# A transformer block on one core: separate PSUM banks for maxima and scores, a one-row shift, two issue tracks for the delta rule, and all weight subtractions on GpSimd

## The chip, the core and the metric

The kernel runs on one core of one Trainium2 chip. A core has TensorE for matrix products (PE in the profile, its weight loads PEld), VectorE (DVE), ScalarE (ACT), GpSimd (POOL) and SyncE, which issues most DMAs (SP). Each engine works through its own list of instructions, in the order in which the program emits them. The metric is the device time of one execution in microseconds (us). Before the change the median of three runs is 3656.62 us (3653.87 to 3657.88).

## The reference

One block of a diffusion transformer: 2048 latent tokens of width 1024, and 256 context tokens. The input is normalised and modulated, projected, and goes through two groups of heads side by side; their outputs are concatenated and projected, and a gated MLP with a width-3 convolution follows.

```
# (a) softmax attention: 8 query heads of 64, 2 key/value heads, blocks of 128 queries
s = einsum("bqkgd,bskd->bkgqs", q_blk, k)        # k: 256 context + 2048 latent keys
p = softmax(s, axis=-1)
o = einsum("bkgqs,bskd->bqkgd", p, v)

# (b) delta rule: 4 heads of 128, forwards and backwards, chunks (64 in the reference)
lower = einsum("bhnid,bhnjd->bhnij", k_beta, k) * decay_strict
t_inv = triangular_solve(lower + eye, eye)       # inverse of a unit triangular matrix
u, w = t_inv @ (v * beta), t_inv @ (k_beta * exp(g_cum))
v_new     = u_n - w_n @ state                    # chunk after chunk
new_state = state * d_n + k_n.T @ v_new
o_n       = q_n @ state + intra @ v_new
```

The inverse of a chunk needs only that chunk's keys and decays. The state goes from chunk to chunk.

## The kernel before, in words

**Stages.** About the first 700 us make the projections, the convolutions and the modulation. The stage that the change touches follows: attention and delta rule together, from about 725 to 1923 us. Then come the output projection and the MLP, which the change leaves alone.

**A planner draws up the order.** In the stage of the change no engine's program is written by hand. `attention` (L1097) and `delta` (L1282) only record operations in a `Plan` (L192). `Plan.cost` (L226) books a duration for each operation: on VectorE 65 ns and the elements at 0.96 per ns, fewer if an input allows a fast mode; on ScalarE 50 ns and 0.836 ns for an element, 42 more if the input lies in SBUF, 93 more if scale or bias is a tensor. `Plan.order` (L303) lays all operations out on the five engines by these durations, by the tiles that are free and by urgency. Every operation belongs to a *track*: `a` (attention), whose urgency is the share of its TensorE work still to do, and `d0` and `d1` (delta rule forwards and backwards), whose urgency is 1.35 (`DW`) times the rest of their longest path. Buffers of one ring are given out in the order of the program within a track (L355). `Plan.issue` (L398) then emits the instructions in the order of their planned starts. That is why nearly all rows of the stage carry line L403 in the profile: operations are told apart by their tiles' names.

**PSUM.** There are 8 banks of 128 x 512 f32. `RINGS` (L44) gives ring `s` two tiles of two banks each, `g` three single banks, `o` one. Scores (`sc`) and the products for the maxima (`sm`, `sm_rest`) both take their tiles from `s`.

**Attention.** 16 query blocks and 2 key heads make 32 groups of 4 heads. For each group `tops` (L1176) first makes a row maximum over all 2304 keys with a one-pass product: eight tiles of 128 x 1024 and a rest, each reduced by VectorE to `mx`, and then `top`. `top` is scaled, split into two f16 parts (`sh6`, `sh2`), turned into rows by TensorE (`tp`) and copied by ScalarE to two rows of `qx` (L1198 to L1210). The score product has two passes, `kh` x `qt` and `kx` x `qx`; the two rows of `qx` meet two constant rows of `kx` and so subtract the maximum. For each of nine score tiles of a group (two key tiles of 128 keys, 512 columns each, L1228) ScalarE makes `p = exp(esc * sc + shift)`, with `esc` and `shift` from tiles. The weights are split in f16: `hp` is the rounded value (VectorE for tiles 0, 3, 6, ScalarE for the others) and `lp = p - hp` (VectorE for tiles 1, 4, 7, `LO_V`, GpSimd for the others). `ops` collects 24 small products for a tile. After each score tile's `exp` one piece of the next group's `tops` is recorded (`next(ahead)`, L1236); what is left of it follows behind the ninth tile.

**Delta rule.** 18 chunks of 128 tokens in each direction. Of every chunk: loads `tT` (keys and queries, turned), `tk` (keys and values) and `rws` (decay rows), one buffer each and direction; decays (`pdb`, `db`), the product of keys (`pkk`), the lower matrix in two f16 parts (`lh`, `ll`), first 2 x 2 inverses (`m0`, `tt`, `t`); then six levels that double the block, each with `py` on TensorE, a masked copy to `y` on VectorE, `pa` on TensorE, and two copies by ScalarE of half of `t` and half of `tt` (L1397, L1398); then one correction step: `it = i16 - t` on VectorE, `pr` on TensorE, `r = it + pr` on VectorE, `pn`, and `ti`, the inverse. The rest is the state: `pw`, `rv`, `pv`, `vn`, `pz`, the new state `s`, and the output `po`. Tiles `ti`, `rv`, `vn`, `o` share a ring of two.

## Time and profile before

| | |
|---|---|
| median of three runs | 3656.62 us (3653.87 to 3657.88) |
| the profiled execution | 3658.18 us |
| its span, first to last instruction | 3656.3 us |
| granted TensorE clock, mean over the span | 0.972 |
| TensorE (PE) busy | 3407.5 us |
| VectorE (DVE) busy | 2466.2 us |
| ScalarE (ACT) busy | 1708.3 us |
| GpSimd (POOL) busy | 1221.0 us |

A row of grouped instructions reads: line, engine, operation, output and inputs by the program's tile names, shapes, count; then busy time in us, mean ns of one; then the idle time of that engine just before them and what ended it. A row of waits reads: who waited, for whom, us in total, times, longest. In a row of a stretch each engine has its busy time and, in brackets, its instructions, and at the end stand granted clock, DMA share and GB/s. Ends of TensorE instructions are modelled in the profile; their starts are measured.

### The profile page before, as it was taken

To read this page: it belongs to the slowest core of one execution; us is meant where nothing else is said; L and a number is where in the kernel's file an instruction comes from. 1 tells how busy PE (TensorE), PEld (TensorE's weight loads), DVE (VectorE), ACT (ScalarE), POOL (GpSimd) and SP (SyncE) were. 2 spreads that over 40 slices of the span, in tenths; PEclk is the share of its full clock that TensorE was granted. 3 is DMA by queue.
4 is the path that set the end of the run, shared out by engine and by line. 5 is a ranking of instruction groups with operands and counts; after the bars stand their busy time and mean duration, and the time that the engine had idled before them with its cause. 6 is when DMAs were issued, how large, how long until landed. Compare 5 with 4: busy or idle time off the path is not lost.

```text
span 3656.3 us, 65344 instructions
## 1 busy us (share of the span) xinstructions
PE 3407.5 (93%) x26245; PEld 2735.9 (75%) x26245; DVE 2466.2 (67%) x3589; ACT 1708.3 (47%) x2772; POOL 1221.0 (33%) x1327
## 2 busy tenths in 40 slices
PE   7899999889989899999887889999999999999998
PEld 3799888766666666666656668888888888888898
DVE  5664778888778887878775657753775376537653
ACT  5442343466667676667663444332433243324331
POOL 4684555434444454544455531100110010001100
PEclk8899999999999999999998999999999999999999
DMA  6222445711111121211105662334333433343333
GB/s 223 85 72 89 137 119 167 211 40 49 62 61 39 56 63 61 65 44 58 58 25 187 222 231 94 98 110 126 117 98 112 125 120 96 113 126 116 98 101 96
DMA packets 209200, 381.31 MB, mean 104 GB/s; under 512 B 20360, under 2 KB 95720, under 8 KB 208624
## 3 DMA queue, kind: packets, MB, share of 16 engines
q1 hardware_dynamic: 207056, 371.74, 32.2%
q0 software_dynamic: 1840, 5.39, 0.6%
q8 instruction: 206, 3.38, 0.4%
q14 instruction: 98, 0.80, 0.1%
HBM read 297.73 MB, written 79.72 MB: 103 GB/s over the span
## 4 chain that ended last, share of the span: by engine, by line
PE 67%; DVE 16%; POOL 5%; DMA 4%; ACT 4%; issue 4%; SPq 0%; POOLq 0%; DVEq 0%; ACTq 0%
PE pu L520 8%; PE pu L521 8%; PE pu L519 8%; PE sc L403 5%; PE pdn L520 4%; PE pdn L521 4%; PE pdn L519 4%; PE ops L403 3%; PE po L403 3%; DVE mx L403 3%; PE sm L403 2%; ACT p L403 2%; DVE lp L403 1%; PE pg L520 1%; PE pg L519 1%
## 5 line engine op out<-in xcount | busy, mean ns | idle before, releaser
L403 POOL TENSOR_TENSOR lp<-p,hp 128x1024 f16<-128x1024 f32 x192 | 412.0, 2146 | 515.3 <-ACT hp L403 246.8
L519 PE MATMUL pu<-h,ws_u 128*128 128x512 f32 x1408 | 552.0, 392 | 2.1 <-ACT h L403 2.1
L520 PE MATMUL pu<-h,ws_u 128*128 128x512 f32 x1408 | 550.3, 391 | 2.5 <-DVE h L403 2.5
L521 PE MATMUL pu<-h,ws_u 128*128 128x512 f32 x1408 | 549.9, 391 | 0.0
L403 ACT ACTIVATE p<-sc,shift,esc 128x1024 f32<-128x1024 f32 x288 | 347.5, 1207 | 171.7 <-PE sc L403 165.3
L403 DVE TENSOR_REDUCE mx<-sm 128x2 f32<-128x1024 f32 x256 | 312.2, 1220 | 74.8 <-PE sm L403 74.1
L1715 POOL COPY carry<-ue 128x2 f32<-128x2 f32 x132 | 24.9, 189 | 893.5 <-ACT ue L1713 893.5
L520 PEld LDWEIGHTS pu<-h,ws_u 128*128 128x128 f32 x1408 | 265.3, 188 | 60.1 <-DVE h L403 4.5
L519 PEld LDWEIGHTS pu<-h,ws_u 128*128 128x128 f32 x1408 | 265.4, 188 | 59.0 <-ACT h L403 3.5
L521 PE MATMUL pdn<-hid,ws_d 128*128 128x512 f32 (+2 forms) x880 | 307.5, 349 | 0.0
L520 PE MATMUL pdn<-hid,ws_d 128*128 128x512 f32 (+2 forms) x880 | 307.5, 349 | 0.0
L521 PEld LDWEIGHTS pu<-h,ws_u 128*128 128x128 f32 x1408 | 265.4, 189 | 55.0
L519 PE MATMUL pdn<-hid,ws_d 128*128 128x512 f32 (+2 forms) x880 | 306.5, 348 | 0.0
L1713 ACT COPY ue<-pu 128x512 f32<-128x512 f32 x176 | 103.2, 587 | 370.1 <-PE pu L521 369.3
L1724 DVE SCALAR_TENSOR_TENSOR cv<-ue,cols,cv 128x512 f32<-128x512 f32 (+1 forms) x352 | 264.9, 753 | 15.8 <-DVE cv L1721 0.5
L403 PE MATMUL sc<-q,kh 128*128 128x512 f16 x576 | 225.0, 391 | 11.4 <-ACT p L403 8.8
L403 PE MATMUL sc<-qx,kx 128*128 128x512 f16 x576 | 225.1, 391 | 2.9 <-ACT qx L403 2.8
L1687 DVE TENSOR_TENSOR ws_u<-raw_u,ws_u 128x1024 fp32r<-128x1024 f32 x176 | 214.6, 1219 | 17.4 <-ACT ws_u L1682 17.4
L1721 DVE TENSOR_SCALAR cv<-ue,cols 128x512 f32<-128x512 f32 (+1 forms) x176 | 96.4, 548 | 190.4 <-ACT ue L1713 188.1
L1687 DVE TENSOR_TENSOR ws_d<-raw_d,ws_d 128x1024 fp32r<-128x1024 f32 (+1 forms) x96 | 109.0, 1136 | 157.7 <-ACT ws_d L1682 155.6
L403 ACT CAST hp<-p 128x1024 f16<-128x1024 f32 x192 | 201.8, 1051 | 5.7 <-PE ops L403 1.5
L403 PE MATMUL ops<-vst,hp 128*128 128x65 f16 (+1 forms) x4608 | 192.1, 194 | 9.0 <-ACT hp L403 6.2
(582 smaller groups left out, 8178.4 us busy)
## 6 DMA issues: line engine op xcount, KB each, us to landing
raw_u<-in_wu SPq DMA_DIRECT2D x176, 512.0 KB
raw_d<-in_wd SPq DMA_DIRECT2D x64, 512.0 KB
tk<-gsc SPq DMA_DIRECT2D x34, 512.0 KB
tT<-gsc SPq DMA_DIRECT2D x66, 256.0 KB
wm<-in_wm SPq DMA_DIRECT2D x64, 256.0 KB
gsc<-kd SPq DMA_DIRECT2D x64, 256.0 KB
raw_o<-in_wo SPq DMA_DIRECT2D x32, 512.0 KB
raw_d<-in_wd SPq DMA_DIRECT2D x32, 384.0 KB
```

Source lines behind the costliest of these rows:

```text
L403: fn(**{k: v.get() if isinstance(v, Lazy) else v for k, v in kw.items()})
L519: PE.matmul(out=ps, lhsT=hi_l(k), rhs=hi_r(k), start=st, stop=False)
L520: PE.matmul(out=ps, lhsT=hi_l(k), rhs=lo_r(k), start=False, stop=False)
L521: PE.matmul(out=ps, lhsT=lo_l(k), rhs=hi_r(k), start=False, stop=en)
L1687: V.tensor_tensor(out=made[u][:, 1, :n], in0=raws[u][:, :n], in1=made[u][:, 0, :n].bitcast(F32), op=ALU.subtract)
L1713: S.copy(out=ue[:, 2:514], in_=ps)
L1715: G.tensor_copy(out=carry[:, b, :], in_=ue[:, 512:514])
L1721: V.tensor_scalar(out=cv[:, :W], in0=ue[:, 0:W], scalar1=fw[0], scalar2=cols[:, C_FB + b:C_FB + b + 1], op0=ALU.mult, op1=ALU.add)
L1724: V.scalar_tensor_tensor(out=cv[:, :W], in0=ue[:, i:i + W], scalar=fw[i], in1=cv[:, :W], op0=ALU.mult, op1=ALU.add)
```

## The change

Seven edits, all in the stage of attention and delta rule but for two scalings of constant rows ahead of it. They come together:

1. **Banks.** Ring `s` has one tile of two banks, for scores alone. A new ring `m` has two single banks, for the maxima: 16 products of 512 columns and 2 rests for a group, each with a reduction of 512 columns, in place of 8 and 1 of 1024.
2. **Recording.** Behind each of the first two score tiles two pieces of `tops` are recorded, so that a group's `tops` ends ahead of its ninth score tile.
3. **Shift.** `top` itself is turned by TensorE, one row in place of two; ScalarE scales it and adds the constant shift when it copies it to one row of `qx`. Four VectorE operations on 128 x 4 values for each group go. Key rows carry the whole scale, so `exp` has a constant scale and no bias.
4. **Subtractions.** `lp = p - hp` is on GpSimd for all nine tiles.
5. **Inverse.** The two copies of a level become one of 512 elements with a strided output. `it` goes; a product with minus the identity (`n16`) puts `-t` into `pr`, and `r = pr + i16`.
6. **Tracks.** What a chunk does up to `ti` is recorded in tracks `i0` and `i1`, the state in `d0` and `d1`, all four with weight 1.35. `tT` and `tk` have two buffers, `ti` a ring of two of its own.
7. **Booked durations.** VectorE 150 ns, 200 more for a fast mode and 55 for a tensor scalar; ScalarE 170 ns, 25 more for an input in SBUF; TensorE 2.34 columns per ns in place of 2.3. This holds in this stage alone.

```diff
-RINGS = dict(s=2, o=1, g=3, p=4, hp=4, lp=4, q=2, h=4, fa=1, at=1, fb=2, tT=1, tk=1, st=2, t=2, fin=1)
+RINGS = dict(s=1, m=2, o=1, g=3, p=4, hp=4, lp=4, q=2, h=4, fa=1, at=1, fb=2, tT=2, tk=2, st=2, t=2, ti=2, rw=1, fin=1)
...
-            return 65 + n / 0.96 / fast + 65 * at, 0.0
+            return fixed[0] + n / 0.96 / fast + fixed[1] * at + (fixed[2] if fast > 1 else 0), 0.0
...
-            return 50 + n * 0.836 + (225 if "accum_out" in kw else 0) + (0 if src(kw["in_"]) else 42) + 93 * at, 0.0
+            return fixed[3] + n * 0.836 + (225 if "accum_out" in kw else 0) + (0 if src(kw["in_"]) else fixed[4]) + 93 * at, 0.0
...
-    plan.patience, plan.rate = PATIENCE, 2.3
+    plan.patience, plan.rate, plan.fixed = PATIENCE, 2.34, (150, 55, 200, 170, 25)
...
+            for h in range(GR):
+                for j in range(4):
+                    sps = psum(f"sm_{nm}_{h}_{j}", "m")
+                    lead(sps, h, 4 * j, 4 * j + 4)
+                    V.tensor_reduce(out=mx[:, h, j:j + 1], in_=sps, axis=AX, op=ALU.max)
+                    if j % 2: yield
             for h in range(0, GR, 2):
-                for j in range(4):
-                    sps = two_banks(f"sm_{nm}_{h}_{j}")
-                    with plan.group():
-                        for i in range(2):
-                            lead(sps[:, i], h + i, 4 * j, 4 * j + 4)
-                    V.tensor_reduce(out=mx[:, h:h + 2, j], in_=sps, axis=AX, op=ALU.max)
-                    yield
...
+                sps = psum(f"sm_{nm}_rest{h}", "m")
...
             V.tensor_reduce(out=top, in_=mx, axis=AX, op=ALU.max)
-            V.tensor_scalar(out=top, in0=top, scalar1=-1.0 / ROWV, scalar2=None, op0=ALU.mult)
...
-            V.tensor_copy(out=sh6, in_=top)
-            V.tensor_copy(out=sh2[:, :, 0], in_=sh6)
-            V.tensor_tensor(out=sh2[:, :, 1], in0=top, in1=sh6, op=ALU.subtract)
...
-                    PE.transpose(out=tps[0:2, h * P:(h + 1) * P], in_=sh2[:, h, :], identity=ident)
-            S.copy(out=qx[0:2, g * GR:(g + 1) * GR, :], in_=tps[0:2, :].rearrange("p (h t) -> p h t", t=P))
+                    PE.transpose(out=tps[0:1, h * P:(h + 1) * P], in_=top[:, h:h + 1], identity=ident)
+            S.activation(out=qx[0:1, g * GR:(g + 1) * GR, :], in_=tps[0:1, :].rearrange("p (h t) -> p h t", t=P),
+                         func=AF.Identity, scale=-1.0 / ROWV, bias=shift[0:1])
...
-                S.activation(out=pr, in_=sps, func=AF.Exp, scale=esc, bias=shift)
-                next(ahead, None)
+                S.activation(out=pr, in_=sps, func=AF.Exp, scale=1.0 / SC)
+                for _ in range(2 if c0 < 4 else 1):
+                    next(ahead, None)
...
-                (V if c0 // 2 in LO_V else G).tensor_tensor(out=lp, in0=pr, in1=hp, op=ALU.subtract)
+                G.tensor_tensor(out=lp, in0=pr, in1=hp, op=ALU.subtract)
...
-    FT = {n: (t, RINGS[t]) for t, ns in (("fa", "db qe"), ("at", "at"), ("fb", "ti rv vn o")) for n in ns.split()}
+    FT = {n: (t, RINGS[t]) for t, ns in (("fa", "db qe"), ("at", "at"), ("ti", "ti"), ("fb", "rv vn o")) for n in ns.split()}
...
+            def two_halves(b):
+                step = 512 + (2 * d - 1) * b
+                x = both_t[:, (1 - d) * b:(1 - d) * b + 2 * step].rearrange("p (a c b) -> p a c b", a=2, b=b)
+                return x[:, :, 0:512 // b - 1:2, :]
...
-                S.copy(out=half(t, b, 1 - d), in_=cols_of(pa[:, 0:256], b))
-                S.copy(out=half(tt, b, d), in_=cols_of(pa[:, 256:512], b))
-            it = f16t("it")
-            V.tensor_tensor(out=it, in0=i16, in1=t, op=ALU.subtract)
+                S.copy(out=two_halves(b), in_=pa.rearrange("p (a c b) -> p a c b", a=2, b=b))
             pr = bank("pr")
             with plan.group():
+                PE.matmul(out=pr, lhsT=n16, rhs=t, start=True, stop=False)
...
-            V.tensor_tensor(out=r, in0=it, in1=pr, op=ALU.add)
+            V.tensor_tensor(out=r, in0=pr, in1=i16, op=ALU.add)
...
+            plan.track = f"d{d}"
             rv = tk[:, 1, :]
...
-            plan.track = f"d{d}"
+            plan.track = f"i{d}"
             next(both[d])
-    plan.issue(dict(a=("work", 1.0), d0=("path", DW), d1=("path", DW, STAG)))
+    plan.issue(dict(a=("work", 1.0), i0=("path", IW), i1=("path", IW, STAG), d0=("path", DW), d1=("path", DW, STAG)))
```

More of the change, by code (lines that the diff above doesn't have):

```diff
@@ L225, in cost @@
     @staticmethod
-    def cost(eng, name, kw, rate):
+    def cost(eng, name, kw, rate, fixed):
         def src(x):
@@ L295, in add @@
             op.behind.add(self.gate)
-        d, a = self.cost(eng, name, kw, self.rate)
+        d, a = self.cost(eng, name, kw, self.rate, self.fixed)
         op.calls.append((fn, kw))
@@ L725, in front @@
         V.tensor_scalar(out=gm, in0=gm, scalar1=1e-15, scalar2=None, op0=ALU.max)
-        ginv = mk(wk, [P, 2], F32, "ginv", "ginv", 1)
-        V.reciprocal(out=ginv, in_=gm)
-        for i, o in enumerate((R_Q, R_K)):
-            V.tensor_scalar(out=rows[:, o:o + HD], in0=rows[:, o:o + HD], scalar1=ginv[:, i:i + 1], scalar2=GTOP,
+        ginv = mk(wk, [P, 1], F32, "ginv", "ginv", 1)
+        V.reciprocal(out=ginv, in_=gm[:, 0:1])
+        for o, by, sc in ((R_Q, ginv, GTOP), (R_K, gm[:, 0:1], SC / GTOP)):
+            V.tensor_scalar(out=rows[:, o:o + HD], in0=rows[:, o:o + HD], scalar1=by, scalar2=sc,
                             op0=ALU.mult, op1=ALU.mult)
@@ L1078 @@
     G.dma_start(out=lv16, in_=k32_d[:, K_LV:K_END])
+    n16 = c2.tile([P, P], F16, name="n16")
+    V.tensor_scalar(out=n16, in0=ident, scalar1=-1.0, scalar2=None, op0=ALU.mult)
     for h in range(HG):
@@ L1135, in attention @@
                             scalar2=None, op0=ALU.mult)
-            V.tensor_scalar(out=kx[0:2, :, g, :], in0=ones[0:2, :].unsqueeze(1).broadcast_to([2, NCK, P]), scalar1=ROWV, scalar2=None, op0=ALU.mult)
+            V.tensor_scalar(out=kx[0:1, :, g, :], in0=ones[0:1, :].unsqueeze(1).broadcast_to([1, NCK, P]), scalar1=ROWV, scalar2=None, op0=ALU.mult)
         for a in range(0, NCK, 6):
             G.dma_start(out=kx[64:128, a:a + 6], in_=ksc[a:a + 6].rearrange("c p f t -> p c f t")[64:128])
-        esc = plan.tile(ak, [P, 1], F32, "esc", "esc", 1)
-        V.scalar_tensor_tensor(out=esc, in0=gm[:, 0:1], scalar=1.0 / GTOP ** 2, in1=gm[:, 1:2], op0=ALU.mult, op1=ALU.mult)
         shift = plan.tile(ak, [P, 1], F32, "shift", "shift", 1)
-        V.tensor_scalar(out=shift, in0=esc, scalar1=-GTOP ** 2 / 128, scalar2=PSHIFT, op0=ALU.mult, op1=ALU.add)
+        V.scalar_tensor_tensor(out=shift, in0=gm[:, 0:1], scalar=8.0 * SC / 1024, in1=gm[:, 1:2], op0=ALU.mult, op1=ALU.mult)
+        V.tensor_scalar(out=shift, in0=shift, scalar1=PSLACK * SC, scalar2=-1.0 / ROWV, op0=ALU.min, op1=ALU.mult)
+        V.tensor_scalar(out=shift, in0=shift, scalar1=PSHIFT * SC / ROWV, scalar2=None, op0=ALU.add)
         vst = plan.tile(ak, [P, NCK, KV, VW], F16, "vst", "vst", 1)
@@ L1182, in lead @@
                 PE.matmul(out=out, lhsT=qt[:, g * GR + h, :], rhs=kh[:, a:b, g, :], start=True, stop=True)
-            for h in range(0, GR, 2):
-                for j in range(4):
-                    sps = two_banks(f"sm_{nm}_{h}_{j}")
-                    with plan.group():
-                        for i in range(2):
-                            lead(sps[:, i], h + i, 4 * j, 4 * j + 4)
-                    V.tensor_reduce(out=mx[:, h:h + 2, j], in_=sps, axis=AX, op=ALU.max)
-                    yield
-            sps = two_banks(f"sm_{nm}_rest")
-            with plan.group():
-                for h in range(GR):
-                    lead(sps[:, h // 2, 256 * (h % 2):256 * (h % 2) + 256], h, 16, NCK)
-            V.tensor_reduce(out=mx[:, :, 4], in_=sps.rearrange("p a (b t) -> p (a b) t", b=2), axis=AX, op=ALU.max)
+            for h in range(GR):
[4 more added lines that the diff above has]
+                    if j % 2: yield
+            for h in range(0, GR, 2):
+                sps = psum(f"sm_{nm}_rest{h}", "m")
+                with plan.group():
+                    for i in range(2):
+                        lead(sps[:, 256 * i:256 * i + 256], h + i, 16, NCK)
+                V.tensor_reduce(out=mx[:, h:h + 2, 4], in_=sps.rearrange("p (b t) -> p b t", b=2), axis=AX, op=ALU.max)
             yield
@@ L1308, in delta @@
             q.dma_start(out=tk, in_=gsc[ck, :, 1 + 2 * d:3 + 2 * d, :])
-            rws = plan.tile(gs, [12, HG, 3, P], BF16, f"rows{d}", f"rows_{nm}", 1)
+            rws = plan.tile(gs, [12, HG, 3, P], BF16, f"rows{d}", f"rows_{nm}", RINGS["rw"])
             q.dma_start(out=rws, in_=rsc[d, ck].rearrange("h r s t -> r h (s t)"))
```

25 lines of the change are left out of this document (12 added, 13 removed).

## The prediction

> **What bounds the kernel now.** The page first, for the span, and then the busy time of the one stage that changes, cut where the delta rule ends.
>
> ```profile
> span 3656.3 us, 65344 instructions
> 725.00:1867.00 1142.00, 1030.58 (x13829) 759.12 (x13830) 920.69 (x1336) 771.21 (x1144) 514.73 (x281) 0.96 0.18 55
> 1867.00:1923.00 56.00, 42.52 (x544) 25.99 (x541) 38.70 (x40) 36.70 (x38) 34.69 (x20) 0.91 0.10 25
> sum 1198.00, PE 1073.10 PEld 785.11 DVE 959.39 ACT 807.91 POOL 549.42; mean PE 536.55 PEld 392.56 DVE 479.70 ACT 403.96 POOL 274.71
> ```
>
> The columns are PE, PEld, DVE, ACT, POOL. The stage takes 1198 us; PE is busy for 1073, DVE for 959, ACT for 808, POOL for 549. The cuts come from two tiles: the last `fin` is the delta rule's last result, the last `p` attention's last score tile.
>
> ```profile
> L403 DVE TENSOR_TENSOR fin<-po,fin x16: 677/691/693, 1352.3 to 1867.0; 128x512 f32<-128x512 f32 x16
> L403 ACT ACTIVATE p<-sc,shift,esc x288: 1190/1204/1280, 751.2 to 1916.5; 128x1024 f32<-128x1024 f32 x144
> ```
>
> So attention ends last, 56 us behind the delta rule. PE is nearest to its limit, with 1198 - 1073 = 125 us idle. The waits of the stage, for PE, say for whom:
>
> ```profile
> PE pt L403 <- DVE t L403: 26.1, 26, 2.4
> PE tp L403 <- DVE sh L403: 23.9, 16, 2.6
> PE pa L403 <- DVE y L403: 11.0, 18, 1.8
> PE sc L403 <- ACT p L403: 8.8, 20, 1.0
> PE sm L403 <- DVE mx L403: 6.6, 13, 1.5
> PE ops L403 <- ACT hp L403: 6.2, 12, 0.9
> PE ops L403 <- POOL lp L403: 5.5, 6, 2.4
> ```
>
> DVE has the largest share, 68 us in four rows. PE's idle time is larger than its rows say, because ends are modelled. The timeline shows it:
>
> ```profile
> 1414.97 0.38 PE L403 MATMUL sc<-q,kh 128*128 128x512 f16 x1
> 1415.19 0.38 PE L403 MATMUL sc<-qx,kx 128*128 128x512 f16 x1
> ```
>
> Products of 512 columns start 0.22 us apart but are drawn 0.38 long; so every wait hides some 0.16 us more. The stage is thus PE work plus waits of PE, and a gain must come out of the waits.
>
> Why DVE is late is in its own rows:
>
> ```profile
> L403 DVE TENSOR_TENSOR m<-lh,lv x36: 409/1072/1943, 740.2 to 1822.5; 128x512 f16<-128x512 f16 x36
> L403 DVE TENSOR_TENSOR t<-i,m x36: 407/1202/2044, 741.7 to 1825.0; 128x512 f16<-128x512 f16 x36
> L403 DVE CAST hp<-p x96: 671/684/1993, 754.2 to 1914.5; 128x1024 f16<-128x1024 f32 x96
> L403 DVE TENSOR_REDUCE mx<-sm 128x2 f32<-128x1024 f32 x256 | 312.2, 1220 | 74.8 <-PE sm L403 74.1
> L403 DVE TENSOR_REDUCE mx<-sm_rest 128x4 f32<-128x1024 f32 x32 | 39.0, 1218 | 4.9 <-PE sm_rest L403 4.7
> L403 DVE TENSOR_TENSOR lp<-p,hp 128x1024 f16<-128x1024 f32 x96 | 134.4, 1400 | 16.9 <-ACT hp L403 14.4 <-POOL lp L403 1.1 <-PE sc L403 0.6
> L403 DVE CAST hp<-p 128x1024 f16<-128x1024 f32 x96 | 73.7, 768 | 7.8 <-ACT p L403 7.6
> L403 DVE TENSOR_TENSOR t<-i,m 128x512 f16<-128x512 f16 x36 | 37.3, 1035 | 0.5
> L403 DVE TENSOR_TENSOR m<-lh,lv 128x512 f16<-128x512 f16 x36 | 36.2, 1005 | 4.3 <-ACT lh L403 4.0
> L403 DVE TENSOR_SCALAR top<-top 128x4 f32<-128x4 f32 x32 | 29.4, 919 | 0.8
> L403 DVE TENSOR_TENSOR it<-i,t 128x512 f16<-128x512 f16 x36 | 27.4, 764 | 2.2 <-ACT t L403 2.2
> L403 DVE CAST sh<-top 128x4 f16<-128x4 f32 x32 | 16.6, 518 | 0.9
> L403 DVE CAST sh<-sh 128x4 f32<-128x4 f16 x32 | 8.1, 253 | 1.0
> L403 DVE TENSOR_TENSOR sh<-top,sh 128x4 f32<-128x4 f32 x32 | 5.0, 156 | 0.0
> L403 DVE TENSOR_REDUCE oss<-osg 128x4 f32<-128x512 f32 x16 | 10.9, 679 | 2.4 <-ACT osg L403 2.4
> L403 POOL TENSOR_TENSOR lp<-p,hp 128x1024 f16<-128x1024 f32 x192 | 412.0, 2146 | 515.3 <-ACT hp L403 246.8 <-DVE hp L403 222.7 <-PE sm L403 28.9
> ```
>
> The first three rows give min/median/max in ns: `m` takes 409 or up to 1943. `top` scales 4 numbers and takes 919 on average. `mx`, which reads PSUM, hardly varies. So some DVE operations that read SBUF alone stand still for up to about 2 us, one POOL subtraction of 2146 ns.
>
> **The change, part by part.** The ACT rows and two chain pieces that it needs:
>
> ```profile
> L403 ACT ACTIVATE p<-sc,shift,esc 128x1024 f32<-128x1024 f32 x288 | 347.5, 1207 | 171.7 <-PE sc L403 165.3 <-POOL tT L403 1.4 <-DVE mx L403 1.3
> L403 ACT CAST t<-pa 128x256 f16<-128x256 f32 x432 | 137.2, 380 | 30.6 <-PE pa L403 28.0
> L403 ACT CAST t<-pt 128x512 f16<-128x512 f32 x36 | 21.0, 583 | 28.6 <-PE pt L403 28.4
> L403 ACT ACTIVATE db<-pdb 128x512 f32<-128x512 f32 x36 | 21.5, 597 | 25.5 <-PE pdb L403 25.4
> L403 ACT CAST hp<-p 128x1024 f16<-128x1024 f32 x192 | 201.8, 1051 | 5.7 <-PE ops L403 1.5
> 1535.74 4.21 DMA osm<-fin
> 1540.44 3.17 DMA tT<-gsc
> ```
>
> *Engine time.* DVE loses `lp` 134, `top` and three `sh` 29 + 17 + 8 + 5 = 59, `it` 27: 220 us. It gains halves of reductions: 32 x 18 = 576 of about 679 ns (row `oss`, also 512 columns) are 391 us against 312 + 39 = 351, so +40. Net -180. POOL gains 96 x 2.146 = 206 and goes to 755 us, 63% of the stage; the DVE operations that stand still for POOL (`m`, `t`, `hp`) then lose more. Their excess is (1005 - 409) x 36 + (1035 - 407) x 36 + (768 - 684) x 96 = 21 + 23 + 8 = 52 us; times 755/549 it is 72, +20. DVE ends near 800 us. ACT: an `exp` of 512 without tensors takes 597, and 256 columns more cost 583 - 380 = 203, so 1024 take 597 + 406 = 1003 in place of 1207, 288 x 0.204 = 59 us less; copies go from 137 (the row's busy time, in which pairs overlap) to 216 x 583 = 126, 11 less. PE gains 36 products of 512 columns, 36 x 0.22 = 8 us.
>
> *On PE's path.* Each term with the value taken and both ends:
> - Shift: four operations (1846 ns for a group) leave the chain `mx`, `top`, `tp`, `qx`, and `tops` ends one score tile earlier, so work lies behind it. Of 23.9 I take -22; ends -27 and 0. If that cover is gone, each group pays `top` to `qx` in full and the 23.9 stay.
> - Maxima: own banks end `sm` waiting behind scores. Of 6.6 I take -5; ends -8 and +10, the latter if the 40 us of longer reductions lie a quarter on the path.
> - Other DVE waits: `pa` <- `y` falls with DVE's load, -6. `pt` <- `t` is set by POOL, and a planner that books 200 ns more puts `pt` later: 0, ends -20 and +18 (the 20 us above).
> - ACT: of `sc` <- `p`, `ops` <- `hp` (15) -10; ends -20 and 0. What is queued behind a late `exp` is `hp` and the copies of a level.
> - Loads of `tT` and `tk` go out a chunk earlier on SP; a chunk's first product no longer waits 3.2 us for a landing, nor behind the store of `fin`. Only some lie on the chain: -4, ends -8 and 0. SP is no bound, the stage's DMA share is 0.18. If `at`, one buffer still, holds the inverse back, the two tracks are one and this term is 0.
> - `n16` +8, in the open on PE, both ends. The constants ahead of the loops are single operations of some 156 ns (the last `sh` row is such a one): 0.
> - About 75 waits that go free 0.16 us each: -12, ends -25 and 0.
> - Order: the planner booked 999 ns for `exp` (row: 1207), 264 for a half copy (380), 1132 for `mx` (1220); it books 683 for a half `mx` (679) and 1051 for `hp` (1051) now. Waits that come of wrong bookings: a fifth of the 78 left, -15; ends -40 and 0.
>
> Sum: -22 - 5 - 6 - 10 - 4 + 8 - 12 - 15 = -66. From the profiled execution's 3658.2 this is 3592.2; the median lies 1.6 lower. Forecast: 3592. The ends sum to about -140 and +30.
>
> A rule of the Trainium skill speaks against edit 4. "SBUF — State Buffer", section "SBUF: two separate sides", says that GpSimd and a VectorE operation with two SBUF inputs or in a two-port mode exclude each other for a whole instruction. The rows of `m` and `top` agree with it, up to 2 us. What it would make of the time is worked out as the third rival below.
>
> **The rivals.**
>
> *DVE paces more than PE's waits tell.* The chain of waits within the stage goes through DVE often:
>
> ```profile
> by line: PE sc L403 14.2%; PE ops L403 9.6%; DVE mx L403 8.1%; PE sm L403 6.0%; DVE lp L403 4.1%; issue 3.9%; ACT p L403 3.9%; PE po L403 3.6%; DVE t L403 2.9%; DVE m L403 2.9%; PE pa L403 2.8%; DVE top L403 2.3%; PE pkk L403 2.3%; PE pz L4
> ```
>
> `lp` and `top` are 6.4% of 1142 us, 73 us, and go; a sixth of `p`'s 45 us is 7; with shift copies and order, 30. Then 3658 - 110 = 3548. Against it: as one link goes, the next wait is seldom far behind.
>
> *Nothing is gained.* The waits that go come back behind other releasers, since PE's stream needs its inputs in a fixed order: 3656. For it: 89% PE busy already.
>
> *POOL holds VectorE up.* With POOL 63% busy, each of 96 `hp`, 36 `m`, 36 `t` meets a running subtraction with chance 0.63 and waits half of it, 168 x 0.63 x 1.07 = 113 us in place of 52. The 61 more fall on operations that PE waits for next (`pt`, `ops`) and eat the gain: 3592 + 61 = 3653, no change. For it: rows `m`, `t`; against: `hp` meets it seldom now, 768 against the 684 above.
>
> *Slower: one score tile.* Scores have a single tile now: four products (0.88 us), a semaphore, `exp` (1.0), a semaphore, and only then the next four. Every 0.1 us that ACT is late at an `exp`, behind an `hp` of 1051 ns, costs PE 288 x 0.1 = 29 us. It decides from 66/288 = 0.23 us a tile; at half an `hp` on three tiles of five, 0.32, the cost is 91: 3592 + 91 = 3683. Against it: with one `tops` piece after each score tile, scores and maxima took turns in the two tiles before, so a score tile already waited for the last `exp`, and `sc` <- `p` is only 8.8 us.
>
> **How the numbers follow.** The forecast (3592, own range 3560 to 3625) gets 0.58, DVE's pace (3548) 0.20, nothing gained and POOL's hold together 0.10 (3656, 3653), the single score tile 0.12 (3683). A measurement of this kernel tells 0.2%, 7 us, from no change. Faster is the first two and a little of POOL's hold, 0.80; same 0.07; slower 0.13. The range reaches into the second and the third case: 3530 to 3650.
>
> **What would show it.** Right: PE's waits for `top` (before: `sh`) under 5 us; DVE near 800 us and POOL near 755 in the stage; `exp` near 1003 ns and one copy of 583; PE busy share over 91%. Wrong: PE waiting for `p` above 40 us in the stage (single tile); `m` and `t` above 1.4 us in the mean, or `ops` waiting for POOL's `lp` above 30 (POOL); the delta rule ending after attention, with PE idle in a tail; or stage time gained and given back behind 1923 us, where nothing changes.

## The result, and the profile after

The changed kernel takes 3515.3 us (median of four, 3510.51 to 3521.07) against 3655.2 us of the kernel before beside it (3653.7 to 3657.9): ratio 0.9617, 95% interval 0.9600 to 0.9634, 140 us less. The prediction had 3592 and a range from 3530 to 3650: the sign was right, the time lies below the range, and the gain is twice the forecast (140 us in place of 66). All times below are medians of executions at the usual clock; one execution of the kernel before (granted clock 0.63) and one of the shift alone (0.84) took much longer and are left out.

The profiled execution spans 3513.9 us. These are the rows of stretches of its trace, the stage first, then its two parts, cut where the delta rule's last `fin` is done:

```profile
725.00:1781.00 1056.00, 1020.21 (x14403) 765.16 (x14404) 794.90 (x1407) 740.99 (x970) 745.14 (x397) 0.99 0.20 62
725.00:1758.00 1033.00, 1006.74 (x14224) 756.21 (x14225) 786.65 (x1398) 729.86 (x955) 725.26 (x383) 0.99 0.20 62
1758.00:1781.00 23.00, 13.47 (x185) 8.95 (x182) 8.25 (x10) 11.13 (x15) 19.88 (x14) 0.82 0.19 47
```

The stage falls from 1198 to 1056 us. Ahead of it lie 725 us in both kernels, and what lies behind its last product stays as it was (1733.7 us before, worked out as the span less the stage's end, and 1733.3 after). So all of the gain is in the stage. TensorE is now idle for 36 us of it by its rows, 125 before; its tail behind the delta rule is 23 us in place of 56. DVE is at 795 and POOL at 745, as forecast.

TensorE's waits in the stage (who waited, for whom, us, times, longest):

```profile
PE ops L403 <- POOL lp L403: 8.8, 7, 4.4
...
PE pt L403 <- DVE t L403: 5.6, 9, 1.4
PE sc L403 <- ACT p L403: 3.9, 11, 0.7
PE sm L403 <- DVE mx L403: 2.4, 6, 1.2
PE pa L403 <- DVE y L403: 1.3, 3, 0.5
```

`tp` (23.9 before) is not among the largest any more, and `pt` <- `t` fell from 26.1 to 5.6, though the prediction gave that wait no gain. In the chain that ended last, over the whole span, VectorE's share fell from 16 to 8% (first before, then after):

```profile
PE 67%; DVE 16%; POOL 5%; DMA 4%; ACT 4%; issue 4%; SPq 0%; POOLq 0%; DVEq 0%; ACTq 0%
PE 77%; DVE 8%; POOL 6%; DMA 4%; issue 3%; ACT 2%; SPq 0%; POOLq 0%; DVEq 0%; ACTq 0%
```

And the groups of the stage that answer those shown of before (busy time, mean ns of one, idle time before them):

```profile
L403 DVE TENSOR_REDUCE mx<-sm 128x1 f32<-128x512 f32 x512 | 336.1, 681 | 74.7 <-PE sm L403 72.6
L403 DVE CAST hp<-p 128x1024 f16<-128x1024 f32 x96 | 96.1, 1001 | 14.0 <-ACT p L403 13.7
L403 DVE TENSOR_TENSOR m<-lh,lv 128x512 f16<-128x512 f16 x36 | 36.9, 1026 | 2.0 <-ACT lh L403 2.0
L403 DVE TENSOR_TENSOR t<-i,m 128x512 f16<-128x512 f16 x36 | 32.9, 915 | 0.3
L403 ACT ACTIVATE p<-sc 128x1024 f32<-128x1024 f32 x288 | 294.9, 1024 | 182.7 <-PE sc L403 173.3 <-POOL lp L403 5.4 <-PE pa L403 1.6
L403 ACT CAST t<-pa 128x512 f16<-128x512 f32 x216 | 124.0, 584 | 48.3 <-PE pa L403 42.8 <-issue 4.4 <-DVE mx L403 0.2
L403 POOL TENSOR_TENSOR lp<-p,hp 128x1024 f16<-128x1024 f32 x288 | 616.0, 2146 | 232.8 <-DVE hp L403 88.0 <-ACT hp L403 52.6 <-issue 19.3
```

The sizes of the operations came out as predicted: 681 ns for a half `mx` (679 forecast), 1024 for `exp` (1003), 584 for the joint copy (583). `hp` on DVE went from 768 to 1001 ns, as a POOL subtraction now runs in 616 of the 1056 us; `m` and `t` hardly moved (1005 to 1026, 1035 to 915).

**The clock.** The kernel before has the granted clock 0.96 in its stage, this one 0.99. In the kernel before the loss comes in pieces. Two neighbouring stretches of 3.4 us of it:

```profile
1029.20:1032.60 3.40, 1.30 (x16) 0.90 (x17) 3.37 (x4) 1.30 (x4) 1.76 (x2) 1.00 0.00 0
1032.60:1036.00 3.40, 3.40 (x47) 2.62 (x46) 2.65 (x5) 2.20 (x5) 2.13 (x1) 0.50 0.03 5
```

In the first, TensorE is busy for 1.30 us; in the second it runs at half clock. Its timeline there, and those of DVE and POOL (start and length in us; in brackets the idle time and what ended it):

```profile
1028.42 0.59 PE L403 MATMUL sm<-kh,q 128*128 128x512 f16 x2
1031.30 0.40 PE L403 MATMUL pt<-i,t 128*128 128x128 f16 x4 [2.29 <-DVE t L403]
...
1033.71 1.04 PE L403 MATMUL sm<-kh,q 128*128 128x512 f16 x2
```
```profile
1028.22 1.73 DVE L403 TENSOR_TENSOR m<-lh,lv 128x512 f16<-128x512 f16 x1
1029.98 1.26 DVE L403 TENSOR_TENSOR t<-i,m 128x512 f16<-128x512 f16 x1
```
```profile
1027.54 2.13 POOL L403 TENSOR_TENSOR lp<-p,hp 128x1024 f16<-128x1024 f32 x1 [3.43 <-ACT hp L403]
1029.62 1.33 POOL L403 TENSOR_TENSOR ll<-db,lh 128x512 f16<-128x512 f32 x1
```

`m`, 0.41 us at its shortest, takes 1.73 and ends 0.3 us behind POOL's subtraction; `t` takes 1.26 and ends 0.3 us behind POOL's `ll`. `pt` waits 2.29 us for it, and then the two products `sm` take 1.04 us in place of 0.59. The records of the granted clock have 17 such pieces (of 3.4 or 6.8 us) between 760 and 1890 us of the kernel before. After the change there are none between 760 us and the delta rule's end at 1758, and two in the tail behind it. Ahead of each of the 17, TensorE's rows show 1.46 to 2.46 us idle in the 3.41 us before; of the 313 other windows of this length only 5 have over 1.5 (windows counted from the moments at which the clock changes). Over the whole stage, with its tail, TensorE was at half clock for 91.7 us before and 28.2 after. While it works at half clock it loses half of the time, so up to (91.7 - 28.2) / 2 = 32 us of the 142 came from the clock; it is an upper bound, since idle time at half clock loses nothing.

"TensorE: Matmul & The Clock Gate" of the Trainium skill, section "HAM oscillation — how this bites in real kernels", gives the rule that idle gaps of more than some 3.4 us are to be kept out. The trace disagrees on the length: 2.29 us in one gap, and 1.46 in a window in all, were enough here.

The account of the stage's 142 us, by rows: TensorE's idle time fell by 89 (125 to 36), its busy time by 53. Of the 53 up to 32 are the clock. The other 21, and 8 more for the `n16` products that were added, are not work that went: they are waits that the drawn ends of products hide. The starts of the products, which are measured, show it. Take as the length of a product the gap to the next start that its kind usually has at full clock (0.215 us for 512 columns), and count longer gaps as standing still, but for what half clock explains. Then the stage's products need 962 us before and 972 after, half clock costs 37 and 7 us more, and TensorE stands still for some 185 us before and 64 after (the rest is gaps of under 0.03 us). So the 142 us are some 121 of waits and 30 of the clock, less 10 of added work. (Other choices of the usual gap raise the standing still by up to 12 us before and 8 after.)

### The profile page after: what moved, and what is told of

It is laid out like the page before. It is cut to its first block, busy times and chain, and to the rows that moved or that the text cites. A ratio compares the mean times of both kernels' runs of the same rounds, so it can differ in the third digit from the quotient of the medians.

```text
span 3513.9 us, 65298 instructions
## 1 busy us (share of the span) xinstructions
PE 3355.6 (95%) x26281; PEld 2715.5 (77%) x26281; DVE 2298.6 (65%) x3619; ACT 1639.6 (47%) x2556; POOL 1410.7 (40%) x1423
## 4 chain that ended last, share of the span: by engine, by line
PE 77%; DVE 8%; POOL 6%; DMA 4%; issue 3%; ACT 2%; SPq 0%; POOLq 0%; DVEq 0%; ACTq 0%
PE pu L520 9%; PE pu L519 9%; PE pu L521 9%; PE sc L403 6%; PE ops L403 5%; PE pdn L521 5%; PE pdn L520 5%; PE pdn L519 5%; PE po L403 3%; PE sm L403 3%; PE pa L403 1%; PE pg L520 1%; PE pg L519 1%; PE pg L521 1%; PE pkk L403 1%
## 5 line engine op out<-in xcount | busy, mean ns | idle before, releaser
L403 POOL TENSOR_TENSOR lp<-p,hp 128x1024 f16<-128x1024 f32 x288 | 616.0, 2146 | 232.8 <-DVE hp L403 88.0
L403 DVE TENSOR_REDUCE mx<-sm 128x1 f32<-128x512 f32 x512 | 336.1, 681 | 74.7 <-PE sm L403 72.6
L1718 POOL COPY carry<-ue 128x2 f32<-128x2 f32 x132 | 24.8, 188 | 891.4 <-ACT ue L1716 891.4
L403 ACT ACTIVATE p<-sc 128x1024 f32<-128x1024 f32 x288 | 294.9, 1024 | 182.7 <-PE sc L403 173.3
L1715 POOL COPY ue<-carry 128x2 f32<-128x2 f32 x176 | 95.4, 543 | 291.6 <-DVE cv L1727 291.3
```

The source lines that it names most:

```text
L403: fn(**{k: v.get() if isinstance(v, Lazy) else v for k, v in kw.items()})
L1715: G.tensor_copy(out=ue[:, 0:2], in_=carry[:, b, :])
L1718: G.tensor_copy(out=carry[:, b, :], in_=ue[:, 512:514])
```

## The experiments

The theory of the prediction: the gain is TensorE's waits for DVE that go, the shift's first. Against it stood that the booked durations and so the order bring most of it; that POOL's load costs part of it; and, once the clock was seen, that what a wait costs is mostly the clock behind it. One kernel does useless products besides. Ratios are to the kernel before. "Stage" is from 725 us to the last product `ops`, "half" the time at half clock in it, both from the trace of one execution; before they are 1197.6 and 91.7, after 1055.6 and 28.2.

### One edit taken out of the changed kernel

**Bookings out.** The old booked durations, all else as changed.

```diff
-    plan.patience, plan.rate, plan.fixed = PATIENCE, 2.34, (150, 55, 200, 170, 25)
+    plan.patience, plan.rate = PATIENCE, 2.3
```

> The changed kernel with the booked durations of before (edit 7 undone, all else kept). If the order was the main thing (theory O: the waits of PE came of wrong bookings), more than half of the 140 us is lost: 3590 us or more, and PE's waits in the stage come back above 80 us. If the freed work of DVE and ACT was the main thing (theory W), at most 40 us is lost: 3555 us or less.

3531.7 us, ratio 0.9659 (0.9640 to 0.9678); stage 1069.6, half 18.3. Last of all, the bookings are worth 16 us, as expected if the freed work was the main thing. Two waits of TensorE grew:

```profile
PE ops L403 <- POOL lp L403: 12.4, 18, 4.4
PE pt L403 <- DVE t L403: 12.0, 15, 1.8
```

**Subtractions shared again.** Three tiles of nine on DVE; 1, 5, 7 in place of 1, 4, 7, the set of before, which no run has alone.

```diff
-                G.tensor_tensor(out=lp, in0=pr, in1=hp, op=ALU.subtract)
+                (V if c0 // 2 in (1, 5, 7) else G).tensor_tensor(out=lp, in0=pr, in1=hp, op=ALU.subtract)
```

> The changed kernel with three of nine subtractions lp back on VectorE (tiles 1, 5 and 7; edit 4 undone, the kernel before had 1, 4 and 7). Theory W: DVE is back at 85 to 90% of the stage and 50 to 90 us are lost, 3565 to 3605. Theory O: the planner books the subtraction on DVE within 15% of its measured time and finds an order nearly as good, 10 to 30 us lost, 3525 to 3545. The rival of POOL's hold: GpSimd back at 46% of the stage, m, t and hp wait less, and the kernel gets faster than 3515.

3518.4 us, 0.9623 (0.9603 to 0.9643); stage 1059.5, half 21.9. The intervals overlap: in the changed kernel it makes no difference that can be told who subtracts, though POOL is busy for 495 of the 940 us from 760 to 1700 in place of 681. None of the three expectations holds it.

**Banks and recording out.** Two-bank tiles of one ring for scores and maxima, as before.

```diff
-RINGS = dict(s=1, m=2, o=1, ...
+RINGS = dict(s=2, o=1, ...
...
-                for _ in range(2 if c0 < 4 else 1):
-                    next(ahead, None)
+                next(ahead, None)
```

> The changed kernel with scores and maxima sharing two tiles of two banks again, maxima in halves no longer, one piece of tops after each score tile (edits 1 and 2 undone). Neither bookings (16 us) nor subtractions (3 us) carry the 140, so the rest must lie in the banks, the shift, the inverse or the tracks. Theory B (banks: scores and maxima held each other up through one ring): 50 us or more lost, 3565 or more, waits of scores for mx and of maxima for mx back. My prediction had 5 us plus a part of the order for it: 3515 to 3535.

3538.8 us, 0.9684 (0.9669 to 0.9699); stage 1079.7, half 21.5. So 24 us, five times the term of the prediction, between the two expectations, and not at the clock. `sm` <- `mx` is 4.6 us in place of 2.4; `sc` <- `p`, which the rival of the single score tile saw growing, is smaller with the single tile (3.9):

```profile
PE ops L403 <- POOL lp L403: 9.2, 18, 1.6
PE sc L403 <- ACT p L403: 5.7, 20, 0.5
PE tp L403 <- DVE top L403: 4.5, 8, 1.5
PE sm L403 <- DVE mx L403: 4.6, 7, 0.9
```

By the starts of its products TensorE stands still 27 us more than in the changed kernel: 9 ahead of `tp`, which waits for `top`, 6 ahead of `ops`, 5 of `sc`, 4 of `sm` and 3 of `py`. No run separates edits 1 and 2, nor, within edit 1, the ring of the maxima's own from the shorter reductions.

**Tracks out.** One track for each direction, one buffer for `tT` and `tk`, `ti` in the ring of `rv`.

```diff
-            plan.track = f"i{d}"
...
-            plan.track = f"d{d}"
             rv = tk[:, 1, :]
...
-    plan.issue(dict(a=("work", 1.0), i0=("path", IW), i1=("path", IW, STAG), d0=("path", DW), d1=("path", DW, STAG)))
+    plan.issue(dict(a=("work", 1.0), d0=("path", DW), d1=("path", DW, STAG)))
```

> The changed kernel with inverse and state of a chunk in one track again, one buffer for tT and tk, ti in the shared ring (edit 6 undone). Theory T (tracks: with one buffer a chunk's inverse could not start before the last chunk's output, so the planner had no delta work to put into PE's gaps): 50 us or more lost, 3565 or more, and PE waiting for t, y and pa again. My prediction had 4 us for it: 3515 to 3530.

3517.9 us, 0.9629 (0.9613 to 0.9645); stage 1055.2. No difference that can be told.

**Inverse out.** Two copies of 256 columns a level, `it` on DVE, no product with `n16`.

```diff
-                S.copy(out=two_halves(b), in_=pa.rearrange("p (a c b) -> p a c b", a=2, b=b))
+                S.copy(out=half(t, b, 1 - d), in_=cols_of(pa[:, 0:256], b))
+                S.copy(out=half(tt, b, d), in_=cols_of(pa[:, 256:512], b))
...
-                PE.matmul(out=pr, lhsT=n16, rhs=t, start=True, stop=False)
```

> The changed kernel with two copies of 256 elements for a level and it on VectorE again, without the product with minus the identity (edit 5 undone). Predicted for it: PE 8 us less and ACT 11 more, within 10 us of the changed kernel: 3505 to 3525. Theory I (the inverse's chain gets shorter and so fits better): 30 us or more lost, 3545 or more.

3515.4 us, 0.9623 (0.9607 to 0.9640); stage 1056.4. No difference that can be told: ScalarE's copies, DVE's `it` and the added products are hidden, or they offset each other.

**Shift out.** Two rows, the four small DVE operations of a group, and `exp` with scale and bias from tiles.

```diff
+            V.tensor_scalar(out=top, in0=top, scalar1=-1.0 / ROWV, scalar2=None, op0=ALU.mult)
+            V.tensor_copy(out=sh6, in_=top)
+            V.tensor_copy(out=sh2[:, :, 0], in_=sh6)
+            V.tensor_tensor(out=sh2[:, :, 1], in0=top, in1=sh6, op=ALU.subtract)
...
-                S.activation(out=pr, in_=sps, func=AF.Exp, scale=1.0 / SC)
+                S.activation(out=pr, in_=sps, func=AF.Exp, scale=esc, bias=shift)
```

> The changed kernel with the two-row shift made by four VectorE operations for a group and exp with tensors for scale and bias again (edit 3 undone). Predicted for it: 22 us and part of 10: about 3540 to 3550, and exp back to 1207 ns. Theory S (shift: four operations that stand still behind a subtraction delay everything): 50 us or more lost, 3565 or more.

3572.4 us, 0.9770 (0.9749 to 0.9792); stage 1112.8, half 48.7. The shift is the largest part: 57 us. And the wait for it is the smaller part of what grows:

```profile
PE sm L403 <- DVE mx L403: 11.7, 17, 2.0
PE sc L403 <- ACT p L403: 10.5, 24, 1.9
PE tp L403 <- DVE sh L403: 9.4, 9, 1.8
```

### The shift, divided

**`exp` alone.** Scale and bias from tiles again, with the values that the changed kernel has as constants.

```diff
-                S.activation(out=pr, in_=sps, func=AF.Exp, scale=1.0 / SC)
+                S.activation(out=pr, in_=sps, func=AF.Exp, scale=esc, bias=zero)
```

> The changed kernel, its values kept, with scale and bias of exp read from tensors again (the half of edit 3 that is on ScalarE). Undoing all of edit 3 cost 56 us. Theory E (exp: 183 ns more in the chain score product, exp, next score product, which has a single tile now, 288 times 0.183 = 53): 35 us or more lost, 3550 or more, score products waiting for p again. Theory V (VectorE's four operations are the main half): at most 15 us lost, 3530 or less.

3512.8 us, 0.9603 (0.9589 to 0.9618); stage 1055.3. ScalarE's load rises by some 45 us in the 940 us from 760 to 1700 (673.44 to 717.94), and nothing is lost: a shorter `exp` is worth nothing that can be told here.

```profile
760.00:1700.00 940.00, 930.70 (x13237) 703.02 (x13235) 710.70 (x1285) 717.94 (x879) 677.96 (x358) 1.00 0.19 60
```

**The four DVE operations alone.** They and the two rows come back, `exp` stays as changed.

```diff
+            V.tensor_scalar(out=top, in0=top, scalar1=-1.0 / ROWV, scalar2=None, op0=ALU.mult)
+            V.tensor_copy(out=sh6, in_=top)
+            V.tensor_copy(out=sh2[:, :, 0], in_=sh6)
+            V.tensor_tensor(out=sh2[:, :, 1], in0=top, in1=sh6, op=ALU.subtract)
```

> The changed kernel, its values kept, with the four VectorE operations on 128 x 4 values and the two-row shift back, exp without tensors (the half of edit 3 that is on VectorE). Theory V: 35 us or more lost, 3550 or more, tp waiting for sh 10 us or more and maxima behind a standing VectorE. Theory E: at most 20 us lost, 3535 or less.

3558.3 us, 0.9727 (0.9708 to 0.9745); stage 1094.2, half 37.9. So 43 of the 57 us (40 by the ratios) are these 128 operations on 4 numbers per partition. The other 14 show only when `exp` has its tensors as well. Their groups:

```profile
L403 DVE CAST sh<-top 128x4 f16<-128x4 f32 x32 | 32.3, 1010 | 0.3
L403 DVE TENSOR_SCALAR top<-top 128x4 f32<-128x4 f32 x32 | 27.3, 854 | 0.3
L403 DVE CAST sh<-sh 128x4 f32<-128x4 f16 x32 | 21.3, 666 | 0.5
L403 DVE TENSOR_TENSOR sh<-top,sh 128x4 f32<-128x4 f32 x32 | 12.5, 391 | 0.0
```

93 us in all, 2.9 us a group, where the kernel before had 59; single ones take from 146 to 2106 ns. Is it that there are four more links in the chain, or that each can stop behind POOL?

**Four links that don't stop.** The same four operations a group, each as a reduction over an axis of one element, a copy; ScalarE scales, and the two rows hold one half each.

```diff
-            V.tensor_scalar(out=top, in0=top, scalar1=-1.0 / ROWV, scalar2=None, op0=ALU.mult)
-            V.tensor_copy(out=sh6, in_=top)
...
+            V.tensor_reduce(out=tb, in_=top.unsqueeze(2), axis=AX, op=ALU.max)
+            V.tensor_reduce(out=sh6, in_=tb.unsqueeze(2), axis=AX, op=ALU.max)
...
```

> As the run before with four VectorE operations back in the shift, but each a reduction over an axis of one element, which only copies (f32, two equal rows at half the scale). In all traces reductions of these sizes take 155 to 176 ns and never stand still. Four operations in a row as before, without the 2 us stops. Theory H (the stops behind POOL's subtractions, not the number of operations): most of the 43 us stays gained, 3535 or less. Theory N (four more links between maximum and scores): 30 us or more lost, 3545 or more.

3520.3 us, 0.9641 (0.9625 to 0.9656); stage 1058.5, half 24.8. Four links that take 147 to 150 ns in the mean, and at most 159, cost some 5 us (0.0024 of 3655 is 9 by the ratios), the four that stop 43:

```profile
L403 DVE TENSOR_REDUCE sh<-tb 128x4 f32<-128x4 f32 x64 | 9.5, 148 | 0.4
L403 DVE TENSOR_REDUCE sh<-sh 128x4 f32<-128x4 f32 x32 | 4.8, 150 | 0.4
L403 DVE TENSOR_REDUCE tb<-top 128x4 f32<-128x4 f32 x32 | 4.7, 147 | 0.2
```

The row of the stretch from 760 to 1700 us has POOL about as busy as after (681.47):

```profile
760.00:1700.00 940.00, 925.14 (x13193) 702.71 (x13193) 728.90 (x1398) 671.05 (x877) 669.23 (x356) 1.00 0.19 61
```

One reservation: the planner books 154 ns for such a reduction and 352 for three of the four others, so the orders differ a little too. The rows agree with "SBUF — State Buffer" of the Trainium skill, section "SBUF: two separate sides", by which only some forms of VectorE's operations share a lock with GpSimd.

### Edits put into the kernel before

**Shift alone.**

```diff
-            V.tensor_copy(out=sh6, in_=top)
...
-                S.activation(out=pr, in_=sps, func=AF.Exp, scale=esc, bias=shift)
+                S.activation(out=pr, in_=sps, func=AF.Exp, scale=1.0 / SC)
```

> The kernel before with edit 3 alone (one-row shift, exp with constants). If edit 3 is worth the same alone as it is on top of the others: 56 us faster than before, about 3600. If it needs the others (a planner that still books 999 ns for exp): 20 us or less faster, 3635 or more. My sum had 22 for the shift and part of 10 for exp: 3625.

3599.5 us (median of three executions), 0.9852 (0.9822 to 0.9882); stage 1142.2, half 42.8. Alone it is worth 54 us by the ratio, as expected if it doesn't need the others; the half clock falls by 49 us, so up to 24 of the 54 are the clock. Its trace still has 23.0 us of `pt` <- `t`:

```profile
PE pt L403 <- DVE t L403: 23.0, 26, 1.8
PE sm L403 <- DVE mx L403: 14.7, 25, 1.9
```

**Bookings alone.**

```diff
-    plan.patience, plan.rate = PATIENCE, 2.3
+    plan.patience, plan.rate, plan.fixed = PATIENCE, 2.34, (150, 55, 200, 170, 25)
```

> The kernel before with nothing but the new booked durations (edit 7 alone; no instruction is added or removed, only their order changes). Theory O: 70 us or more faster than before, 3585 or less. Theory W: within 25 us of before, 3630 to 3670, as DVE at 80% leaves no better order. My sum had 15 us for it: 3640.

3622.1 us, 0.9905 (0.9887 to 0.9923); stage 1161.1, half 55.2. 35 us for six numbers that run on no engine, between the two expectations; half as much again as `tp`'s whole wait. The half clock falls by 36.5 us, so up to 18 of the 35 are the clock. `pt` and `tp` fall to a third (from 26.1 and 23.9):

```profile
PE pa L403 <- DVE y L403: 11.5, 18, 2.0
PE sc L403 <- ACT p L403: 11.3, 29, 0.7
PE pt L403 <- DVE t L403: 8.9, 11, 1.2
...
PE tp L403 <- DVE sh L403: 7.6, 7, 2.0
```

**Bookings and all subtractions on POOL.**

```diff
+    plan.patience, plan.rate, plan.fixed = PATIENCE, 2.34, (150, 55, 200, 170, 25)
...
-                (V if c0 // 2 in LO_V else G).tensor_tensor(out=lp, in0=pr, in1=hp, op=ALU.subtract)
+                G.tensor_tensor(out=lp, in0=pr, in1=hp, op=ALU.subtract)
```

> The kernel before with the new booked durations and all subtractions on GpSimd (edits 4 and 7). Theory W: 60 to 100 us faster than before, 3555 to 3595, and clearly faster than edit 7 alone. Theory O: no more than 25 us beyond edit 7 alone. POOL's hold: slower than edit 7 alone.

3641.2 us, 0.9961 (0.9947 to 0.9976); stage 1179.9, half 74.0. Edit 4 costs 19 us on top of the bookings, as expected of POOL's hold. Its trace bears that out in part: `t` on DVE takes 879 ns in the mean in place of 739, the cast `sh` 636 in place of 213, and `pt` <- `t` grows from 8.9 to 17.9 us. But `ops` also waits longer for POOL's own `lp` (8.1 to 14.7), and no run separates the two.

**Shift and bookings; then banks as well.**

Edits 3 and 7 as in the two above, then edit 1 and 2 as well.

```diff
+    plan.patience, plan.rate, plan.fixed = PATIENCE, 2.34, (150, 55, 200, 170, 25)
...
+                S.activation(out=pr, in_=sps, func=AF.Exp, scale=1.0 / SC)
```

> The kernel before with the shift (edit 3) and the booked durations (edit 7). Alone they brought 52 and 35 us. If they add up: 87 us, 3568. If both remove the same waits: 60 us or less, 3595 or more.

```diff
+RINGS = dict(s=1, m=2, o=1, ...
...
+                for _ in range(2 if c0 < 4 else 1):
+                    next(ahead, None)
```

> The kernel before with own banks, earlier recording, shift and booked durations (edits 1, 2, 3 and 7; subtractions, inverse and tracks as before). Undone singly, subtractions, tracks and inverse cost 2 to 4 us each. If they are worth as little together: 3515 to 3530. If they can stand in for each other, so that undoing one shows nothing: 3540 or more.

3582.1 us, 0.9808 (0.9792 to 0.9824), and 3538.1 us, 0.9689 (0.9673 to 0.9705); stages 1117.9 and 1073.1, half 31.9 and 19.8. Shift and bookings together bring 1.92% where their single gains add up to 2.43%: each takes part of what the other would. Edits 1 and 2 add 44 us to these two, so 114 of the 140 are edits 1, 2, 3, 7.

**The rest in pairs.** Inverse and tracks out of the changed kernel together; then subtractions (1, 4, 7 on DVE) and inverse.

```diff
-            plan.track = f"i{d}"
...
+                S.copy(out=half(t, b, 1 - d), in_=cols_of(pa[:, 0:256], b))
+                S.copy(out=half(tt, b, d), in_=cols_of(pa[:, 256:512], b))
```

> The changed kernel with inverse and tracks as before together (edits 5 and 6 undone, subtractions all on GpSimd). Singly each cost 2 to 4 us, with the subtractions as a third about 25 together. If inverse and tracks stand in for each other: 15 us or more lost, 3530 or more. If not: 10 or less, 3525 or less.

```diff
+                (V if c0 // 2 in (1, 4, 7) else G).tensor_tensor(out=lp, in0=pr, in1=hp, op=ALU.subtract)
...
+                S.copy(out=half(t, b, 1 - d), in_=cols_of(pa[:, 0:256], b))
```

> The changed kernel with subtractions (tiles 1, 4 and 7 on VectorE) and inverse as before together (edits 4 and 5 undone, tracks split). Both put work back on VectorE, which would then be near 86% of the stage. If the two stand in for each other: 15 us or more lost, 3530 or more. If not: 10 or less.

3532.2 us, 0.9654 (0.9639 to 0.9668), and 3526.2 us, 0.9642 (0.9624 to 0.9661). Taken out one by one, edits 4, 5 and 6 show 3, 0 and 3 us; 5 and 6 together show 14 by the ratios (0.0037 of 3655), and all three against edits 1, 2, 3, 7 alone 26 (0.0072). So they seem to stand in for each other. It isn't sure: the three together exceed their single losses (9 us by the ratios) by 17, and the intervals of the five kernels leave that uncertain by about as much. Which work would do so is open.

### The clock by itself

**Useless products.** The kernel before, with three products of 512 columns more ahead of each `pt` and each `tp`, 204 in all, into tiles that are overwritten next. They have no other purpose than to keep TensorE at work while it waits.

```diff
             pt = bank("pt0")
+            for _ in range(3):
+                PE.matmul(out=pt, lhsT=id16, rhs=m0, start=True, stop=True)
...
             tps = psum(f"tp_{nm}", "g")
+            for _ in range(3):
+                PE.matmul(out=tps[0:GR], lhsT=sh6, rhs=i16, start=True, stop=True)
```

> The kernel before with useless products on PE, three of 512 columns ahead of each pt and each tp, into the bank that the real product then overwrites: 204 products, 44 us of added PE work, put where PE waited for t and for sh. In the trace of before PE's granted clock was at half for 17 stretches of 3.4 or 6.8 us between 760 and 1890 us, each behind a window of 3.4 us in which PE's rows show over 1.4 us idle. Theory C (idle windows cause the half clock): with the waits filled there are 10 or fewer such stretches, and part of the 44 us comes back, 3685 or less. If the half clock has nothing to do with idle windows: 15 or more stretches remain.

3650.6 us, 0.9981 (0.9971 to 0.9992); half 57.1 us in place of 91.7, 7 pieces in place of 17. 204 products at 0.22 us are 45 us of work, and the kernel is no slower, but 0.2% faster. The same 940 us, first before, then with the useless products:

```profile
760.00:1700.00 940.00, 855.22 (x11616) 635.49 (x11614) 758.48 (x1109) 641.42 (x960) 434.57 (x238) 0.97 0.18 56
```
```profile
760.00:1700.00 940.00, 879.45 (x11820) 640.09 (x11820) 757.19 (x1115) 643.60 (x966) 439.08 (x239) 0.99 0.18 56
```

In this stretch there are 204 products more too, but by chance: 168 of them are useless ones (93 ahead of `pt`, 75 ahead of `tp`), so the useful work is all but the same. Filling the waits took away 10 of the 17 pieces, as expected if idle windows bring the half clock. By the starts of the products TensorE stands still 30 us less in the stage and loses 16 us less to half clock, together about what was added. So the clock is a cost of its own, apart from the wait, and pays here for a third of the products; the idle time that they fill pays for the rest. One reservation: the planner places the useless products too, so the order differs a little.

### A version beyond both

The changed kernel without the `n16` product (`it` on DVE again), and with every other subtraction of the last group on DVE, to shorten the tail of 23 us.

```diff
-                PE.matmul(out=pr, lhsT=n16, rhs=t, start=True, stop=False)
+            V.tensor_tensor(out=it, in0=i16, in1=t, op=ALU.subtract)
...
+                (V if n + 1 == len(groups) and c0 // 2 % 2 else G).tensor_tensor(out=lp, in0=pr, in1=hp, op=ALU.subtract)
```

> The changed kernel without the product with minus the identity (it = i16 - t on VectorE again, one copy for a level kept), 8 us less on PE, and with every second subtraction of the very last group on VectorE, where GpSimd alone held PE up for 8.8 us. PE is busy for 97% of the stage, so its work is what is left: 8 to 14 us faster than the changed kernel, 3501 to 3508, if VectorE's new operation is hidden; no gain if it stands still behind POOL and PE waits for r.

3519.1 us, 0.9635 (0.9621 to 0.9650); stage 1054.9. No gain: TensorE is busy 8 us less in the stage (1012 for 1020), and it waits longer:

```profile
PE ops L403 <- POOL lp L403: 10.5, 10, 2.9
PE pt L403 <- DVE t L403: 7.2, 10, 1.4
```

No version beats the changed kernel by more than the interval.

## Why the prediction was right, and where it failed

The forecast, 3592, was 77 us too slow, and 3515 lies outside its range: the way was right, the size was not. Right were the bound (TensorE's stream plus its waits), the place (all in the stage), the sizes of the operations, DVE near 800 and POOL near 755 us, and what was to show it: no large wait for `top`, TensorE's share above 91% (1020 / 1056 is 97%). The single score tile is refuted: `sc` <- `p` went from 8.8 to 3.9 us. "Nothing is gained" is refuted as well. "DVE paces more than PE's waits tell" (3548) had the right thought, that `top` on the chain costs more than the waits put down to it, but it priced links by their share of the chain, and it falls short by 33 us; `lp` on DVE, its larger half, is worth nothing that can be told. POOL's load costs 19 us on top of the bookings, and nothing that can be told in the full change.

The prediction's terms for waits add up to -74 us and `n16` to +8. By the starts of the products the waits fell by some 121 us, the clock, for which there is no term, gave 30, and the work grew by 10. The steps that failed, in the prediction's words:

- *"Shift: ... Of 23.9 I take -22; ends -27 and 0."* Measured 54 alone and 57 as the last edit, beyond the end. The step costed only what TensorE waits at `tp`. But the four operations hold up DVE for 59 us before the change, and 93 in the changed kernel with them put back, and what is queued behind them is late too: by the starts TensorE stands still some 35 us longer with them back, 16 ahead of `tp`, 7 ahead of `sm` and the rest spread. The prediction had the row that shows it, `top` at 919 ns, and used it only for the chain to `qx`. That it is their stops and not the length of the chain is shown by the four reductions (5 to 9 us lost in place of 43).
- *The clock.* The window row with 0.96 is in the prediction's first fence, and no term uses it. It is worth 30 us, and it is not a term beside the others: where 1.46 us or more were idle in one window of 3.41 us, half clock followed in 17 of 23 cases for the next one or two, and a piece of 3.41 us at half clock costs up to 1.7 us. So each term that ends long waits was too small.
- *"About 75 waits that go free 0.16 us each: -12, ends -25 and 0."* The waits fell by some 121 us by the starts and by 89 as drawn, so some 32 us were hidden in drawn ends, beyond the end. The prediction saw that ends hide waits, and sized it too small.
- *"Order: ... a fifth of the 78 left, -15; ends -40 and 0."* 35 alone (up to 18 of it the clock), 16 as the last: within its ends, and the value taken was low for the edit alone.
- *"Maxima: ... Of 6.6 I take -5; ends -8 and +10."* 24 as the last edit (with edit 2), 44 on top of shift and bookings. What is gained isn't the wait of `sm`: with banks shared it is 2.2 us longer, and the four rows shown are some 9 us longer together. By the starts the 24 are waits too, 9 us of them ahead of `tp` and the rest spread. How the shared banks bring them is not explained by these runs.
- *"`pt` <- `t` is set by POOL ...: 0, ends -20 and +18."* It went from 26.1 to 5.6; with bookings alone, which change nothing but the order, it is 8.9 already. `m` still takes 1000 ns in the mean there and 1026 in the changed kernel: it stops as long, and TensorE waits for it less. POOL's load does count, within the end: with all subtractions on POOL the 8.9 become 17.9.
- *"ACT: ... -10; ends -20 and 0."* Nothing that can be told: the kernel with `exp` with tensors again takes no longer (0.9603), and the one with two copies a level neither (0.9623).
- *Tracks -4, `n16` +8.* Tracks show 3 us by themselves, within the ends. The `n16` products are drawn as 8 us of busy time; taken out, with `it` on DVE again, they bring no time, as TensorE then waits longer. So the 8 us are not simply "in the open on PE".

The edits don't add up. One by one out of the changed kernel they show 57 + 24 + 16 + 3 + 3 + 0 = 103 of 140 us; in the kernel before, shift and bookings show less together than singly. Open are how the shared banks make TensorE wait, whether and how edits 4, 5, 6 cover for each other, and the exact idle time from which the clock falls.

## What to carry to other kernels

Where TensorE runs dry for short stretches, read the granted clock by pieces of a few us beside its idle time: here 1.46 us or more of idle time in 3.41 us was mostly followed by half clock, which adds to what the wait itself costs, and a forecast from waits alone was too small. A tiny VectorE operation is to be costed with its mean and its longest time and with what stands behind it on its engine: 128 operations on four numbers were worth 43 us, as they stopped for up to 2.1 us beside a busy GpSimd, and the same number as reductions that never stopped 5 to 9. Count waits by the starts of products where the ends are modelled: here the drawn ends hid some 32 us of the gain. A static order is only as good as the durations it is made from: six booked numbers brought 35 us with no operation changed.

## What the hardware showed that was not expected

- TensorE's clock fell to half for one or two pieces of 3.41 us after windows of 3.41 us in which it had been idle for only 1.46 to 2.46 us in all (five such windows with 1.68 to 1.84 us were not followed by it); 45 us of useless products that cut these pieces from 17 to 7 made the kernel no slower.
- A VectorE reduction of 4 values that reads SBUF takes 147 to 150 ns beside a GpSimd that is busy for 71% of the stretch (669 of 940 us), while, in the kernel that has them, a cast of 4 values takes 1010 ns in the mean.
- `exp` of 1024 columns takes 1207 ns with scale and bias from tiles and 1024 with constants, 183 ns apart, and 288 of these made no difference to the time that can be told.
